# A hybrid decoder step: stream buffers and gate matrices allocated later, attention emitted in larger steps

## The chip, the cores and the metric

The kernel runs on one core of one Trainium2 chip. The metric is the device time of one execution in microseconds (us). The kernel before was timed three times: 1510.71, 1504.4 and 1509.47 us, so the median is 1509.47 us. One more execution was profiled: it took 1513.5 us, of which the trace covers a span of 1511.7 us.

Engines are named as the profile names them: PE is the matrix engine (PEld its weight loads), DVE the vector engine, ACT the scalar engine, POOL GpSimd, SP the engine that here only issues transfers.

## The reference, cut to what matters

One layer for 256 prompt tokens and 32 new tokens of 8 running sequences (288 columns in all):

```
h = RMSNorm(x);  [p_rwkv | lru_x | lru_gate | q | k | v] = h @ W_in
y = concat(RWKV7(p_rwkv), RGLRU(lru_x, lru_gate), DilatedWindowAttn(q, k, v)) @ W_out
x = x + RMSNorm(y)
x = x + RMSNorm(relu(RMSNorm(x) @ W1)^2 @ W2)
```

The attention has 8 heads of 128 numbers and a bias that depends on the distance of query and key alone. For the prompt it is a block form: query block 0 sees key block 0, query block 1 sees key blocks 0 and 1. For the running sequences it reads 896 of the 2048 cached keys and values of each sequence, those that the dilated windows reach. The RWKV part has 8 heads of 64 in two halves of four; a half is a chain of small dependent matrix products.

## The kernel before, in words

**Dense work.** Every weight chunk of 512 KB is loaded by SP, split by ACT and DVE into a high and a low part (L385, L386, three ring slots), and multiplied on PE three times (L421 high by high, L422 high by low, L423 low by high). One such product with 288 columns is called a dense matmul here. The input projection has 46 output tiles of 48 dense matmuls each (2208 in all); then the output projection runs in four passes of 192 (R, L, G0, G1: the RWKV part, the LRU part, heads 0 to 3, heads 4 to 7), then the feed-forward layer with 6144. Places in the program are given as *tile 29*, that is, after 29 x 48 dense matmuls, counted on from the input projection into the passes, so that pass R begins at tile 46, L at 50, G0 at 54, G1 at 58.

**Mixers.** What lies between the projections (RWKV, LRU, attention) is written as Python generators. While the dense work is emitted, `pump` runs them a step at a time within a budget, so that their instructions stand between the dense ones; a scheduler then sets the final order on every engine, and each engine runs its own list in that order. Before a pass the program drains the generators that the pass needs. `yield 0.85` tells `pump` what a step costs.

**RWKV.** `gen_rwkv(hf)` prepares half `hf`; `gen_form` makes its 64 x 64 products; `gen_inv` inverts blocks on DVE and turns them by a round trip through DRAM (DVE copy L851, out with L854, back with L859, all on SP's queue), whose result PE needs in `gen_mats` (L888). `gen_chain`, `gen_rwkv_sample` and `gen_gn` follow. The constant `GATE` names the key of half 0 that half 1 waits for before it starts at all: `Q1`, set when half 0 has finished the second of its two `gen_mats`.

**Cached keys and values.** `gen_sample_scores` takes 32 batches of keys of 896 KB (L1365, issued by POOL, four matmuls L1395 each), `gen_sample_pv` 32 half batches of values of 1024 or 768 KB (L1458, 28 matmuls L1479 for a whole batch). They share four stream buffers: two in `arm` and two taken from the arena at the start (`ar` in the trace). POOL issues in order: a load whose buffer isn't free holds up what stands behind it.

**Prompt attention.** `gen_prompt_attn` runs head by head. The bias is a table by distance; a load gives it in the order of growing distance, so that it is turned around on PE by two transposes with a reversed identity (`jm`, L1544) and evicted by ACT (L1545), then scores (L1555, L1556), softmax, three transposes (L1576). `gen_prompt_pv` turns the values (L1593) and multiplies (L1600, L1601), head by head.

**The end.** After the last column sums (`sum_cols`, L404) and ahead of the last scaling stands a loop of 72 matmuls (L1814) whose results nobody reads.

Of the kernel before, what the change touches and what calls it, by code (L numbers as in the profile page):

```python
# [17 lines left out]
NT = NP_ + NS  # L18
# [33 lines left out]
GATE = 'Q1'  # L52
# [41 lines left out]
def _consts():  # L94
# [50 lines left out]
    return ca, cb, oh_p, ln_p, oh_s, ln_s, np.eye(128, dtype=np.float32)[::-1].copy()  # L145
# [17 lines left out]
def prepare(inputs):  # L163
# [58 lines left out]
    a["c_a"], a["c_b"], a["c_ohp"], a["c_lnp"], a["c_ohs"], a["c_lns"], a["c_j"] = _consts()  # L222
# [89 lines left out]
def build(tc, A, O):  # L312
    nc = tc.nc
    sy, dv, ac, po, pe = nc.sync, nc.vector, nc.scalar, nc.gpsimd, nc.tensor
    with ExitStack() as ctx:
# [337 lines left out]
        def gen_rwkv(hf):  # L653
# [528 lines left out]
        def gen_lru():  # L1182
# [3 lines left out]
            gt = yield from aw(2, 4, 128)  # L1186
            sy.dma_start(out=gt, in_=A["gates"])
# [25 lines left out]
            yield 0  # L1213
            while 0 not in xbt:
                yield 0
# [83 lines left out]
        def evac_qkv(which, i, ps):  # L1299
# [5 lines left out]
            QKV[which, i] = t  # L1305
            S[which + "n"] = i + 1
# [3 lines left out]
        def gen_tables():  # L1310
# [17 lines left out]
            jm = yield from aw(128)  # L1328
            sy.dma_start(out=jm, in_=A["c_j"])
            S["jm"] = jm  # L1330
# [21 lines left out]
        def gen_sample_scores():  # L1352
# [3 lines left out]
            def pre(n):  # L1356
                for i in range(n):
# [13 lines left out]
            for g in range(2):  # L1371
# [12 lines left out]
                for hf in range(2):  # L1384
                    bh, = yield from bk(1)
                    for b in range(NB):
                        i = (g * 2 + hf) * NB + b
                        pre(i + 1 + LAG)
                        yield from take()
                        while i not in kst:  # L1390
                            yield 0
                            pre(i + 1)
                        t, buf = kst[i]
                        for h in range(4):
                            pe.matmul(out=bh[32 * h:32 * h + 32, 0:448], lhsT=qz[:, h, b], rhs=t[:, h],  # L1395
                                      start=(b == 0), stop=(b == NB - 1))
                        streams.append(buf)
                        kst[i] = None
                        yield 0.85
# [43 lines left out]
        def gen_sample_pv():  # L1443
# [3 lines left out]
            def pre(n):  # L1447
                for i in range(n):
# [12 lines left out]
            for g in range(2):  # L1461
# [4 lines left out]
                for b in range(NB):  # L1466
                    bb, = yield from bk(1)
                    for kg in range(2):
                        i = (g * NB + b) * 2 + kg
                        pre(i + 1 + LAG)  # L1470
                        yield from take()
                        while i not in vst:
                            yield 0
                            pre(i + 1)
                        t, buf = vst[i]
# [6 lines left out]
                        vst[i] = None  # L1482
                        if kg == 0:
                            yield 1.2
# [6 lines left out]
                    yield 1.0  # L1491
# [30 lines left out]
        def gen_prompt_attn():  # L1522
            while "dtab" not in S:
                yield 0
            d0, jm = S["dtab"], S["jm"]
            hbs = {}

            def load(h):
                t = yield from aw(2, 128)
                for i in range(2):  # L1530
                    po.dma_start(out=t[:, i], in_=bass.AP(tensor=d0.tensor, offset=d0.offset + 384 * h + 1 + 128 * i,
                                                          ap=[[1, 128], [1, 128]]))
                hbs[h] = t

            yield from load(0)
            for _ in range(6):
                yield 0
            for h in range(8):
                TB = yield from aw(256)
                if h < 7:  # L1540
                    yield from load(h + 1)
                b, = yield from bk(1)
                for i in range(2):
# [3 lines left out]
                arena.put(hbs.pop(h))  # L1547
                while ("k", h) not in QKV:
                    yield 0
                qt, kt = QKV.pop(("q", h)), QKV.pop(("k", h))  # L1550
                P = yield from aw(3, 128)
                s_ = yield from aw(8)
                yield 0.2
                b, = yield from bk(1)
                pe.matmul(out=b[:, 0:128], lhsT=qt[:, 0:128], rhs=kt[:, 0:128], start=True, stop=True)  # L1555
                pe.matmul(out=b[:, 128:384], lhsT=qt[:, 128:256], rhs=kt[:, 0:256], start=True, stop=True)  # L1556
                near, far = TB[:, 0:128], TB[:, 128:256]
                for blkq, tb in ((0, near), (1, far), (2, near)):
                    dv.scalar_tensor_tensor(out=P[:, blkq], in0=b[:, 128 * blkq:128 * blkq + 128], scalar=SCALE, in1=tb,
                                            op0=ALU.mult, op1=ALU.add)  # L1560
                banks.put(b)
                arena.put(TB, qt, kt)
                sls = (slice(0, 1), slice(1, 3))
                for i, sl in enumerate(sls):
                    dv.tensor_reduce(out=s_[:, i:i + 1], in_=P[:, sl], axis=mybir.AxisListType.XY, op=ALU.max)
                dv.tensor_scalar(out=s_[:, 0:2], in0=s_[:, 0:2], scalar1=-1.0, scalar2=None, op0=ALU.mult)
                for i, sl in enumerate(sls):
                    ac.activation(out=P[:, sl], in_=P[:, sl], func=AF.Exp, bias=s_[:, i:i + 1], accum_out=s_[:, 2 + i:3 + i])
                dv.reciprocal(out=s_[:, 4:6], in_=s_[:, 2:4])
                for i, sl in enumerate(sls):  # L1570
                    dv.tensor_scalar(out=P[:, sl], in0=P[:, sl], scalar1=s_[:, 4 + i:5 + i], scalar2=None, op0=ALU.mult)
                yield 0.7
                PT = yield from aw(3, 128)
                b, = yield from bk(1)
                for i in range(3):
                    pe.transpose(b[:, 128 * i:128 * i + 128], P[:, i], ident)  # L1576
                ac.activation(out=PT, in_=b[:, 0:384].rearrange("p (a b) -> p a b", a=3), func=AF.Copy)
                banks.put(b)
                arena.put(P, s_)
                QKV["p", h] = PT  # L1580
                yield 0.4
            arena.put(jm)

        def gen_prompt_pv():
            outs = {}
# [255 lines left out]
```

## Time and profile before

| | |
|---|---|
| three runs | 1504.4 to 1510.71 us, median 1509.47 us |
| the profiled execution: its time, its span | 1513.5 us, 1511.7 us |
| PE | busy 1447.7 us (96% of the span) |
| PEld | 1358.9 us (90%) |
| DVE | 837.0 us (55%) |
| ACT | 604.2 us (40%) |
| POOL | 80.1 us (5%) |
| HBM | 268.03 MB read, 6.84 MB written, 182 GB/s over the span |
| the chain that ended last | PE 90%, DMA 4%, DVE 3%, ACT 1%, issue 1% |

The averages hide stages. The profile's view in 40 slices has a slice of 37.8 us each; the feed-forward layer fills the slices from 18 on evenly, and slices 12 and 13 (from about 453 to 529 us) stand out on PE, on PEclk (the granted clock of PE, 9 for full speed, 5 for half) and on DMA. A matmul's end is modelled, so a busy PE says how long it had work in flight, not that it ran at its peak; the rate of the dense matmuls is the better measure.

### The profile page before, as it was taken

The page shows a single profiled execution, that of the slowest core. Times are in us where ns is not written, and L with a number is a line of the kernel's source. Part 1 is how long each engine was busy: PE and PEld are TensorE (multiplying, and loading weights), DVE is VectorE, ACT ScalarE, POOL GpSimd, SP SyncE. Part 2 cuts the span into 40 slices and gives each one's busy share as a digit, 9 for nine tenths or more (in the row PEclk, how much of TensorE's full clock was granted, in tenths as well). Part 3 has the DMA queues.
Part 4 walks back from the last instruction along what each step waited for, and adds up shares of the span by engine and source line. Part 5 has one row for each costly group of instructions (what it writes and reads, how often), then busy time and mean ns, then how long its engine had stood idle before and what let it go on. Part 6 is the DMA issues. An engine that isn't in the chain of part 4 may idle for free.

```text
span 1511.7 us, 28221 instructions
## 1 busy us (share of the span) xinstructions
PE 1447.7 (96%) x11802; PEld 1358.9 (90%) x11802; DVE 837.0 (55%) x1415; ACT 604.2 (40%) x880; POOL 80.1 (5%) x167
## 2 busy tenths in 40 slices
PE   9998999999997769999999999999999999999997
PEld 8897778778886439999999999999999999999996
DVE  7785348447775146679443345544455544455554
ACT  7432325334433114366443344433344433444442
POOL 3101012121111000000000000000000000000000
PEclk9999999999998559999999999999999999999998
DMA  8656576787986114534544444444454454444452
GB/s 302 180 158 197 184 286 229 266 337 269 348 265 208 41 34 167 183 126 154 163 162 166 167 166 168 166 165 165 164 165 167 168 167 165 164 162 165 168 168 77
DMA packets 86319, 276.70 MB, mean 183 GB/s; under 512 B 22528, under 2 KB 26288, under 8 KB 84144
## 3 DMA queue, kind: packets, MB, share of 16 engines
q1 hardware_dynamic: 75280, 212.30, 41.4%
q0 software_dynamic: 10048, 60.84, 11.3%
q8 instruction: 92, 1.51, 0.4%
q10 hardware_dynamic: 864, 1.77, 0.3%
q14 instruction: 35, 0.29, 0.1%
HBM read 268.03 MB, written 6.84 MB: 182 GB/s over the span
## 4 chain that ended last, share of the span: by engine, by line
PE 90%; DMA 4%; DVE 3%; ACT 1%; issue 1%; POOL 0%; SPq 0%; DVEq 0%; ACTq 0%; POOLq 0%
PE mm L421 26%; PE mm L422 26%; PE mm L423 26%; PE bt L1479 2%; PE bt L1395 2%; DMA ar<-do 1%; DMA w<-in_w_in 1%; DMA ar<-dtab 1%; DMA o_v<-ar 1%; DMA arm<-in_vc 1%; PE bt L965 0%; PE bt L1070 0%; PE bt L1083 0%; DVE arm L1818 0%; DMA ar<-dm 0%
## 5 line engine op out<-in xcount | busy, mean ns | idle before, releaser
L386 DVE TENSOR_TENSOR ring_l<-w,ring_h 128x1024 fp32r<-128x1024 f32 (+1 forms) x382 | 465.2, 1218 | 395.1 <-ACT ring_h L385 392.7
L385 ACT ACTIVATE ring_h<-w 128x1024 fp32r<-128x1024 f32 (+1 forms) x382 | 403.0, 1055 | 578.1 <-PE mm L422 528.5
L421 PE MATMUL mm<-hh,ring_h 128*128 128x288 f32 x1984 | 598.8, 302 | 3.8 <-ACT ring_h L385 2.0
L422 PE MATMUL mm<-hl,ring_h 128*128 128x288 f32 x1984 | 592.7, 299 | 0.2 <-DVE hl L540 0.2
L423 PE MATMUL mm<-hh,ring_l 128*128 128x288 f32 x1984 | 589.9, 298 | 0.0
L421 PEld LDWEIGHTS mm<-hh,ring_h 128*128 128x128 f32 x1984 | 374.5, 189 | 15.2 <-issue 8.3
L423 PEld LDWEIGHTS mm<-hh,ring_l 128*128 128x128 f32 x1984 | 375.4, 189 | 6.9 <-issue 5.2
L422 PEld LDWEIGHTS mm<-hl,ring_h 128*128 128x128 f32 x1984 | 375.1, 189 | 5.4 <-issue 3.1
L422 PE MATMUL mm<-fl,ring_h 128*128 128x288 f32 x1024 | 302.1, 295 | 0.0
L423 PE MATMUL mm<-fh,ring_l 128*128 128x288 f32 x1024 | 301.9, 295 | 0.0
L421 PE MATMUL mm<-fh,ring_h 128*128 128x288 f32 x1024 | 300.3, 293 | 0.0
L421 PEld LDWEIGHTS mm<-fh,ring_h 128*128 128x128 f32 x1024 | 192.5, 188 | 0.0
L422 PEld LDWEIGHTS mm<-fl,ring_h 128*128 128x128 f32 x1024 | 192.5, 188 | 0.0
L423 PEld LDWEIGHTS mm<-fh,ring_l 128*128 128x128 f32 x1024 | 192.4, 188 | 0.0
L1781 ACT ACTIVATE fh<-ft 128x288 fp32r<-128x288 f32 x64 | 28.3, 445 | 78.9 <-DVE ft L1780 78.9
L1789 DVE TENSOR_TENSOR arm<-mm,arm 128x288 f32<-128x288 f32 x48 | 22.0, 458 | 51.1 <-PE mm L423 51.1
L1782 DVE TENSOR_TENSOR fl<-ft,fh 128x288 fp32r<-128x288 f32 x64 | 29.2, 458 | 29.2 <-ACT fh L1781 29.2
L1780 DVE SCALAR_TENSOR_TENSOR ft<-mm,rt 128x288 f32<-128x288 f32 x63 | 28.3, 450 | 0.0
L1779 ACT ACTIVATE rt<-mm 128x288 f32<-128x288 f32 x63 | 24.9, 395 | 0.4 <-PE mm L423 0.4
L1479 PE MATMUL bt<-arm,ar 128*32 128x128 f32 x472 | 19.2, 317 | 5.4 <-DVE ar L848 2.5
L1479 PEld LDWEIGHTS bt<-arm,ar 128*32 128x32 f32 x472 | 14.7, 126 | 8.1 <-DVE ar L848 2.7
L1688 DVE TENSOR_TENSOR ar<-mm,ar 128x288 f32<-128x288 f32 x32 | 14.6, 455 | 8.8 <-PE mm L423 8.8
(438 smaller groups left out, 992.9 us busy)
## 6 DMA issues: line engine op xcount, KB each, us to landing
w<-in_w SPq DMA_DIRECT2D x256, 512.0 KB
w<-in_w_in SPq DMA_DIRECT2D x91, 512.0 KB
w<-in_w_out SPq DMA_DIRECT2D x32, 512.0 KB
arm<-in_kc POOLq DMA_DIRECT2D x16, 896.0 KB, 6.6
ar<-in_kc POOLq DMA_DIRECT2D x16, 896.0 KB, 7.6
ar<-in_vc POOLq DMA_DIRECT2D x8, 1024.0 KB, 7.0
arm<-in_vc POOLq DMA_DIRECT2D x8, 1024.0 KB, 6.5
arm<-in_vc POOLq DMA_DIRECT2D x9, 768.0 KB, 6.8
```

The costliest lines, as they stand in the source:

```text
L385: ac.activation(out=h[:, lo:hi], in_=t[:, lo:hi], func=AF.Copy)
L386: dv.tensor_tensor(out=l[:, lo:hi], in0=t[:, lo:hi], in1=h[:, lo:hi].bitcast(F32), op=ALU.subtract)
L421: pe.matmul(out=ps, lhsT=h, rhs=xh, start=start, stop=False)
L422: pe.matmul(out=ps, lhsT=h, rhs=xl, start=False, stop=False)
L423: pe.matmul(out=ps, lhsT=l, rhs=xh, start=False, stop=stop)
L1395: pe.matmul(out=bh[32 * h:32 * h + 32, 0:448], lhsT=qz[:, h, b], rhs=t[:, h], start=(b == 0), stop=(b == NB - 1))
L1479: pe.matmul(out=bb[32 * h:32 * h + 32, 0:128], lhsT=PT[:, kt, 32 * h:32 * h + 32], rhs=t[:, q, h], start=(kt == 0), stop=(kt == 6))
L1779: ac.activation(out=r, in_=ps, func=AF.Relu)
L1780: dv.scalar_tensor_tensor(out=f, in0=ps, scalar=0.0, in1=r, op0=ALU.max, op1=ALU.mult)
L1781: ac.activation(out=fh[:, m], in_=f, func=AF.Copy)
L1782: dv.tensor_tensor(out=fl[:, m], in0=f, in1=fh[:, m].bitcast(F32), op=ALU.subtract)
L1789: dv.tensor_tensor(out=facc[:, m], in0=ps, in1=facc[:, m], op=ALU.add)
```

## The change

- **RWKV half 1 starts earlier.** `GATE` becomes `TQ`, the key that half 0 sets when its inversion has been emitted.
- **Stream buffers late.** At the start there are only the two in `arm`. `more_streams` takes the other two from the arena once half 1 of RWKV has its last large buffer (the key `held`).
- **Gate matrices late.** `gen_lru` takes memory for the gate matrices and loads them once the first tile of values has left PE (the key `late`).
- **Cached keys in twos.** `gen_sample_scores` waits for two batches and emits their eight matmuls in one step; each of the two stands for one `take`.
- **Cached values by batch.** `gen_sample_pv` waits for both halves of a batch and emits its 28 matmuls in one step.
- **Prompt heads in pairs, keys backwards.** The bias is loaded for two heads by two transfers of 128 KB and used as it comes: the scores are made with the keys in reverse (`kt[:, 127::-1]`), and the softmax's last step writes them forwards again. `jm`, its two transposes per head and the eviction are gone. Softmax and values run two heads at a time; a head's product with the values is three matmuls of 128 columns (before: one of 256 and one of 128).
- **The loop of 72 matmuls at the end is gone.**

```diff
-GATE = 'Q1'
+GATE = 'TQ'
-        streams = [arm[:, 0:2304], arm[:, 2304:4608]] + [arena.get(2048, top=True) for _ in range(NSTR)]
-        strx = streams[2:]
+        streams = [arm[:, 0:2304], arm[:, 2304:4608]]
+        strx = []
+        def more_streams():
+            while "held" in RS[1] and len(strx) < NSTR:
+                t = arena.get(2048, top=True)
+                if t is None:
+                    return
+                strx.append(t)
+                streams.append(t)
...
             MV = yield from aw(2, NT, top=True)
+            R["held"] = True
...
+            while "late" not in S:
+                yield 0
+            gt = yield from aw(2, 4, 128)
+            sy.dma_start(out=gt, in_=A["gates"])
...
-                    for b in range(NB):
-                        i = (g * 2 + hf) * NB + b
-                        pre(i + 1 + LAG)
-                        yield from take()
-                        while i not in kst:
+                    for b2 in range(0, NB, 2):
+                        i = (g * 2 + hf) * NB + b2
+                        for _ in range(2):
+                            yield from take()
+                            pre(i + 2 + LAG)
+                        while i not in kst or i + 1 not in kst:
                             yield 0
...
-                b, = yield from bk(1)
-                for i in range(2):
-                    pe.transpose(b[:, 128 * i:128 * i + 128], hbs[h][:, i], jm)
-                ac.activation(out=TB, in_=b[:, 0:256], func=AF.Copy)
...
+                    pe.matmul(out=b[:, 0:128], lhsT=qt[:, 0:128], rhs=kt[:, 127::-1], start=True, stop=True)
+                    pe.matmul(out=b[:, 128:384], lhsT=qt[:, 128:256], rhs=kt[:, 255::-1], start=True, stop=True)
...
-        for n, K in ((6, 128), (6, 64), (6, 32), (6, 128), (6, 32)):
-            for i in range(n):
-                for r in range(128 // K):
-                    pe.matmul(out=bt[:, r, 0:NT], lhsT=ring_h[K * r:K * r + K, 0, i], rhs=F["h"][K * r:K * r + K, i],
-                              start=True, stop=True)
```

The order on the engines moves at three places. Line numbers of the changed program are eight higher up to the attention, then more.

PE, pass R just after the input projection, before. L1083 to L1151 are the last steps of RWKV half 1, and the rows above them are the same kind of work with few dense matmuls between:

```order
L1003 MATMUL bt<-ar_88 64x64 x4
L1083 MATMUL bt<-ar_88 64x64 x4
L1098 MATMUL bt<-ca,ar_88 64x32 x4
L1128 MATMUL bt<-ar_88,ca 128x288 x2
L1135 MATMUL bt<-ar_88,ca 128x288 x2
L1110 MATMUL bt<-ar_88 64x512 x2
L1151 MATMUL bt<-ar_88 128x288 x2
L421 MATMUL mm<-hh,ring_h 128x288 x3
L422 MATMUL mm<-hl,ring_h 128x288
```

The same pass in the changed program; L1494 are a batch of cached values, L429 to L431 the dense matmuls:

```order
L429 MATMUL mm<-hh,ring_h 128x288
L430 MATMUL mm<-hl,ring_h 128x288
L431 MATMUL mm<-hh,ring_l 128x288
L1494 MATMUL bt<-ar_88 32x128 x16
L1494 MATMUL bt<-arm,ar_88 32x128 x12
L429 MATMUL mm<-hh,ring_h 128x288
```

What moved: from tile 45.9 to tile 46.6 PE's list holds 347 mixer matmuls in the program of before and 4 in the changed one. There RWKV half 1 ends at tile 39.6, the LRU's last gate products stand at 43.4, and the last batch of values at tile 50.0.

PE, the first matmuls of RWKV half 1 that need the round trip through DRAM, in the changed program (L1445 is the softmax of the cached scores, L897 the consumer of the round trip, L1561 and L1562 scores of prompt heads):

```order
L431 MATMUL mm<-hh,ring_l 128x288
L1445 MATMUL bt<-ca,arx 128x128 x4
L897 MATMUL bt<-ar_88 64x64 x16
L1561 MATMUL bt<-ar_88,arx 128x128
L1562 MATMUL bt<-ar_88,arx 128x256
```

They stood at tile 44.9 and stand at tile 29.0 now. Between VectorE's copy that starts the round trip and the consumer, PE's list holds 65 dense matmuls in the program of before (for either half) and 41 dense and 14 other matmuls for half 1 in the changed one (66 dense for half 0).

POOL, the loads of cached keys for heads 0 to 3, before (L1304 is the copy that belongs to the eviction of a tile):

```order
L1365 DMA arm<-in_kc 128x1792
L1304 COPY arx<-ar_88 128x32
L1365 DMA arm<-in_kc 128x1792
L1365 DMA ar_88<-in_kc 128x1792 x2
L1304 COPY arx<-ar_88 128x32
L1365 DMA arm<-in_kc 128x1792
```

and in the changed program:

```order
L1315 COPY arx<-ar_88 128x32 x2
L1376 DMA arm<-in_kc 128x1792 x4
L1315 COPY arx<-ar_88 128x32
L839 MEMSET ar_88 128x1024
L1376 DMA arm<-in_kc 128x1792 x2
L1315 COPY arx<-ar_88 128x32
L1376 DMA arm<-in_kc 128x1792 x2
```

All 32 key batches go through the two buffers in `arm` now; the loads into the other two begin at tile 35.4, with values. The pairs of key batches stand at tiles 20.2, 21.4, 22.3, 22.9, 24.2, 25.2, 26.0 and 27.2, then (after one batch of values at 29.5 in the same two buffers) at 30.3, 30.9, 31.8, 33.0, 34.1, 34.8, 35.6 and 36.3.

## Rows read from the trace of the kernel before

**Rows 1.** The page, 40 slices: busy tenths of PE, granted clock.

```profile
PE   9998999999997769999999999999999999999997
PEclk9999999999998559999999999999999999999998
```

**Rows 2.** Stretches: start:end us, length, busy of each engine (instructions), clock, DMA.

```profile
core 0: us, PE busy (x) PEld busy (x) DVE busy (x) ACT busy (x) POOL busy (x), PEclk, DMA share, GB/s
149.00:252.60 103.60, 103.48 (x995) 77.81 (x994) 55.99 (x120) 36.24 (x60) 18.35 (x36) 1.00 0.68 245
252.60:451.00 198.40, 190.46 (x1876) 161.74 (x1874) 130.84 (x306) 77.25 (x132) 33.20 (x66) 0.98 0.81 286
463.50:565.00 101.50, 69.55 (x706) 46.28 (x705) 39.51 (x103) 20.84 (x48) 3.60 (x8) 0.61 0.25 81
565.00:660.00 95.00, 95.00 (x708) 93.91 (x708) 64.41 (x102) 45.35 (x69) 0.00 (x0) 1.00 0.50 168
680.00:1490.00 810.00, 810.00 (x6102) 809.79 (x6102) 407.16 (x483) 342.52 (x452) 0.00 (x0) 1.00 0.48 162
```

**Rows 3.** The same view, two short stretches behind waits.

```profile
140.00:160.00 20.00, 18.84 (x229) 16.84 (x230) 6.62 (x12) 5.42 (x10) 1.55 (x3) 0.86 0.46 158
320.00:340.00 20.00, 18.11 (x125) 14.06 (x117) 6.38 (x14) 6.21 (x13) 3.86 (x6) 0.91 0.80 291
```

**Rows 4.** PE groups, 463.5 to 565 us: count, busy, mean ns, idle before.

```profile
L1479 PE MATMUL bt<-arm,ar 128*32 128x128 f32 x136 | 7.3, 387 | 1.3 <-ACT ar L920 0.5 <-ACT ar L966 0.5 <-DVE ar L1041 0.4
L1479 PE MATMUL bt<-ar 128*32 128x128 f32 x112 | 5.2, 349 | 1.0 <-ACT ar L1245 1.0
```

**Rows 5.** PE groups, 149 to 252.6 us.

```profile
L422 PE MATMUL mm<-hl,ring_h 128*128 128x288 f32 x129 | 40.8, 316 | 0.0
L423 PE MATMUL mm<-hh,ring_l 128*128 128x288 f32 x129 | 40.0, 310 | 0.0
L421 PE MATMUL mm<-hh,ring_h 128*128 128x288 f32 x128 | 39.6, 310 | 0.0
```

**Rows 6.** The chain that ended last, pieces: start us, us, what.

```profile
204.48 0.89 PE bt L1395 x8
375.83 1.01 PE bt L1479 x32
```

**Rows 7.** PE's waits in the whole span: us in total, times, longest.

```profile
PE bt L888 <- DMA ar<-do: 6.7, 1, 6.7
PE bt L1395 <- ACT ar L1545: 1.9, 1, 1.9
PE bt L1544 <- DMA ar<-dtab: 1.5, 2, 1.1
```

**Rows 8.** VectorE's copies that start the two round trips: start, us.

```profile
126.85 0.37 DVE L851 COPY ar<-ar 64x256 f32<-64x256 f32 x1
...
442.50 0.39 DVE L851 COPY ar<-ar 64x256 f32<-64x256 f32 x1
```

**Rows 9.** The chain behind the first round trip, and SP's issues of the second.

```profile
127.54 2.41 DMA do<-ar
131.60 9.41 DMA ar<-do
141.15 0.45 PE bt L888 x2
...
447.32 3.77 SPq L859 DMA_DIRECT2D ar<-do  x8
```

**Rows 10.** The line of key loads: POOL's time of one, and landing.

```profile
L1365 POOL DMA_DIRECT2D arm<-in_kc x16: 530/530/536, 128.7 to 315.6; - x16
...
DMA to landing us min/median/max: 4.6/7.4/12.1
```

**Rows 11.** PE forms of the bias transposes and of the scores: ns min, median, max.

```profile
L1544 PE MATMUL bt<-arx,ar x14: 272/328/331, 250.3 to 340.4; 128*128 128x128 f32 x14
...
L1556 PE MATMUL bt<-ar x8: 379/380/382, 274.4 to 345.6; 128*128 128x256 f32 x8
```

**Rows 12.** The end of the kernel in time: ACT's last square, then PE.

```profile
1494.02 0.44 ACT L1792 ACTIVATE sqt<-arm 128x288 f32<-128x288 f32 x1 [5.33 <-DVE arm L1789]
...
1494.13 1.36 PE L1814 MATMUL bt<-fh,ring_h 128*128 128x288 f32 x8
1495.43 0.83 PE L404 MATMUL mm<-ca,sqt 128*128 128x1 f32 x6
```

More of the change, by code (lines that the diff above doesn't have):

```diff
@@ L144, in _consts @@
     ln_s = np.tile(ln_s, (4, 1))
-    return ca, cb, oh_p, ln_p, oh_s, ln_s, np.eye(128, dtype=np.float32)[::-1].copy()
+    return ca, cb, oh_p, ln_p, oh_s, ln_s
 OUTS = {
@@ L1305, in evac_qkv @@
             QKV[which, i] = t
+            if which == "v":
+                S["late"] = True
             S[which + "n"] = i + 1
@@ L1385, in gen_sample_scores @@
                     bh, = yield from bk(1)
-                    for b in range(NB):
-                        i = (g * 2 + hf) * NB + b
-                        pre(i + 1 + LAG)
-                        yield from take()
-                        while i not in kst:
-                            yield 0
[L1392 to L1399, printed above, removed]
+                    for b2 in range(0, NB, 2):
[4 more added lines that the diff above has]
+                        while i not in kst or i + 1 not in kst:
+                            yield 0
+                            pre(i + 2)
+                        for b in (b2, b2 + 1):
+                            t, buf = kst[i + b - b2]
+                            for h in range(4):
+                                pe.matmul(out=bh[32 * h:32 * h + 32, 0:448], lhsT=qz[:, h, b], rhs=t[:, h],
+                                          start=(b == 0), stop=(b == NB - 1))
+                            streams.append(buf)
+                            kst[i + b - b2] = None
+                        yield 1.7
                     sl = SS[:, g, 448 * hf:448 * hf + 448]
@@ L1467, in gen_sample_pv @@
                     bb, = yield from bk(1)
-                    for kg in range(2):
[L1469 to L1475, printed above, removed]
+                    i = (g * NB + b) * 2
+                    for _ in range(2):
+                        yield from take()
+                        pre(i + 2 + LAG)
+                    while i not in vst or i + 1 not in vst:
+                        yield 0
+                        pre(i + 2)
+                    for kg in range(2):
+                        t, buf = vst[i + kg]
                         for q in range((4, 3)[kg]):
@@ L1524, in gen_prompt_attn @@
                 yield 0
[L1525 to L1526 removed]
+            d0 = S["dtab"]
+            tabs = {}
             def load(h):
[L1529 to L1535 removed]
@@ L1582, in gen_prompt_attn @@
[L1582 to L1602 removed]
+                t = yield from aw(2, 2, 128)
@@ new lines, in gen_prompt_pv @@
+        def gen_prompt_pv():
+            for h0 in range(0, 8, 2):
+                while ("v", h0 + 1) not in QKV or ("p", h0) not in QKV:
+                    yield 0
+                PT = QKV.pop(("p", h0))
+                VP = yield from aw(2, 2, 128)
+                b, = yield from bk(1)
+                for e in range(2):
+                    vt = QKV.pop(("v", h0 + e))
+                    for j in range(2):
+                        pe.transpose(b[:, 256 * e + 128 * j:256 * e + 128 * j + 128], vt[:, 128 * j:128 * j + 128], ident)
+                    arena.put(vt)
+                ac.activation(out=VP, in_=b.rearrange("p (e j d) -> p e j d", e=2, j=2), func=AF.Copy)
+                banks.put(b)
+                yield 0.6
+                o0 = yield from att_out(h0)
+                o1 = yield from att_out(h0 + 1)
+                b, = yield from bk(1)
+                for e in range(2):
+                    o = 256 * e
+                    pe.matmul(out=b[:, o:o + 128], lhsT=VP[:, e, 0], rhs=PT[:, e, 0], start=True, stop=True)
+                    pe.matmul(out=b[:, o + 128:o + 256], lhsT=VP[:, e, 0], rhs=PT[:, e, 2], start=True, stop=False)
+                    pe.matmul(out=b[:, o + 128:o + 256], lhsT=VP[:, e, 1], rhs=PT[:, e, 1], start=False, stop=True)
+                for e, oh in enumerate((o0, o1)):
+                    ac.activation(out=oh[:, 0:256], in_=b[:, 256 * e:256 * e + 256], func=AF.Copy)
```

125 lines of the change are left out of this document (53 added, 72 removed).

## The prediction, made before the changed kernel ran

> **What bounds the kernel now.** I read the 40 slices first. PE is at 9 nearly throughout, but slices 12 and 13 show 7 on PE and 8 and 5 on its clock [rows 1]. Then the stretches [rows 2]: in the feed-forward layer PE runs 6102 matmuls in 810.00 us, 0.1327 us each, at clock 1.00. Nothing in the change touches that, so over half of the time is fixed. The stretch from 463.5 to 565 us is the other extreme: 101.50 us long, PE busy 69.55 us, clock 0.61, which is a mix of its two levels of 2.4 and 1.2 GHz. In it PE runs only 31 dense matmuls; the rest is RWKV half 1, some four batches of cached values, four prompt heads and the LRU's last product. Here nothing is full: DVE is busy 39.51 us, the DMA share is 0.25. PE waits for short dependent steps, 32 us in all, and the idle time brings the low clock, so that the steps themselves take twice as long. The same steps for RWKV half 0 stand from 149 to 252.6 us between dense matmuls, and there PE is busy 103.48 of 103.60 us at clock 1.00 [rows 2]. So the bound of this stretch is the latency of a chain with no dense work to fill its gaps. That is what the moved `GATE` changes: in the new order half 1 ends at tile 39.6, well inside the input projection, and the value batches run on to tile 50.0 inside the passes that don't need them.
>
> **The change part by part.** All sums are against the profiled execution, 1513.5 us.
>
> *The pile-up.* The work stays on PE's list; what goes is idle time and low clock. At full clock it would cost at least 69.55 x 0.61 = 42.4 us [rows 2]. From the other side I price it by half 0: 103.60 us less 386 dense matmuls [rows 5] at 0.1327 us (51.2) leaves 52.4 us; in it are 16 key batches at 0.89 us [rows 6], 14.2 us, and about 2 us of other products, so half 0 cost 36 us. Part of half 1's first products had run before 463.5 us (about 2.5 us), so 33.5. To that come 31 dense matmuls (4.1), 248 records of values, where 32 took 1.01 us, so 8 [rows 4, 6], and prompt heads and LRU (5): 50.6 us. I take 46.5, the middle, as neither side is nearer. The pile-up gives back 55 us (bounds 51 and 59).
>
> *The second round trip.* For half 0, PE needs the result at 141.15 us, and the copy ends at 127.22, so the trip takes 13.9 us [rows 8, 9]; 65 dense matmuls (8.6 us) stand in between, and PE waits 6.7 us [rows 7]. In the program of before half 1 had as much cover and no long wait: its copy ends at 442.89, SP issues the last return at about 451.1 [rows 8, 9], so a trip of over 8.2 us with less traffic. In the new order half 1 has 41 dense matmuls (5.4 us) and 14 others, about 1.7 us: 7.1 us. PE, which takes its list in order, waits between 1 and 6.8 us there with all dense work behind it. I take 5. Behind half 0's wait the clock is 0.86 over 20 us [rows 3], which costs 2.8 us; I add 3. Together +8 (0 to 10).
>
> *Keys and values.* A pair holds both buffers until its own matmuls are through. From its start to the next pair's data pass 2 x 0.89 us, POOL's 0.53 us and a landing of 7.4 us (4.6 to 12.1) [rows 6, 10]: 9.7 us. Half 0's stretch ran 8.05 tiles in 103.60 us, 12.9 us a tile [rows 2, 5], so the pairs' distances of 0.63 to 1.25 tiles are 8.1 to 16 us, and of the 15 pairs that follow another batch three wait, 0.5 to 1.6 us each: +3. One pair (tile 34.1) is late for another reason: its loads stand on POOL's list behind the copy of a tile evicted at 33.5. With that, and some value batches that stand half a tile apart at tile 40, I take +6 in all, clock included (0 to 61, the upper end under the rivals).
>
> *The bias.* 16 transposes leave PE, 0.33 us of span each but overlapped [rows 11], about 2 us; the 1.5 us wait for the table goes, and the 1.9 us wait of a key batch behind ACT's eviction L1545 [rows 7], with the clock of 0.91 about it, 1.8 us [rows 3]. The table's load still has to land, but at a DVE instruction now. I take -5 (0 to -7). Reversed keys and the reversed write change an address step alone; no row shows such an access. Between nothing and a doubling of the 16 score matmuls at 0.33 to 0.38 us a span [rows 11], 5 us, I take 0, as the count of columns is the same. Eight more value matmuls: +1.
>
> *The end.* ACT's square is ready at 1494.46; PE's sums of it start at 1495.43, behind eight of the unread matmuls [rows 12]. That is -0.9; the other 64 stand where the scaling or DVE's tail is later anyway.
>
> *Late buffers and gate matrices, other load.* The gate load lands some tiles ahead of its use at tile 38: nothing. DVE takes 39.51 us more into the mixed part [rows 2]: 55.99 + 130.84 + 39.51 = 226.3 us of some 350 us, 65%, so it isn't the bound on the mean; for local queues +2. What is late next: R, L and G0 have their inputs 2.6 tiles and more ahead, G1 7 tiles.
>
> Sum: -55 + 8 + 6 - 5 + 1 - 0.9 + 2 = -44, so 1469.5 us for an execution like the profiled one. The median of the three runs stands at 1509.47/1513.5 = 0.9973 of it: 1465 us.
>
> **The rivals.**
>
> *DVE or the chains bind in places.* In the new order half 1's shift mixing stands about tile 21 and the LRU about tile 40, both long on DVE, beside the splits that DVE owes the dense work. Already in the stretch from 252.6 to 451 us DVE is busy 66%, and PE is idle 7.94 us [rows 2]. If PE waits there as long as half of the pile-up's 32 us of idle time [rows 2], 16 us, and 4 us of clock follow, the gain is 24 us: 1485. For it: half 1 is a chain of small steps with the same latencies as before. Against it: half 0's stretch has 0.12 us of idle time.
>
> *Slower: the key pairs serialise.* A load that always lands in 12.1 us, the longest seen [rows 10], makes a pair's cycle 14.4 us. Summed over the distances, ten of the pairs then wait 43 us, and behind each wait comes low clock, 1.8 us each as about 320 us [rows 3], 18 us: 61 instead of the 6 in the sum, so +11, 1520 us. It decides from a landing of about 11 us on. Against it: such landings came where four loads were queued at once, and now there are never more than two.
>
> The Trainium skill speaks for this rival in Trainium Kernel Development and Optimization, Best Practices: double-buffer, so that loads overlap with compute. A pair that takes both buffers isn't double-buffered. By that rule the waits are those of this rival; by the rows the next pair stands far enough behind that dense work covers the load, and the sum keeps +6. TensorE: Matmul & The Clock Gate, the section on HAM oscillation, adds that a loop with a transfer wait in every step runs every step cold, as the clock of 0.86 and 0.91 behind two waits here has it for single ones.
>
> *Nothing is gained.* The change could leave the pile-up if memory ran out and a drain emptied the generators at the end of the projection. The new order speaks against it: 4 mixer matmuls stand there.
>
> *More is gained.* The lower price of the pile-up, no new waits and the bias at its best: -59 - 7 - 0.9 = -67, 1443 us.
>
> **How the numbers follow.** The forecast, 1465, has a chance of 0.65; DVE and chains, 1485, 0.18; more, 1443 to 1450, 0.10; nothing 0.03; slower 0.04. The range of 8 in 10 goes from 1445 (most of the better case) to 1489 (the DVE rival with a little more wait); it leaves out the last two cases and the edges. About 0.5%, 7.5 us, is what a measurement of this kernel can tell from no change. Faster by more: 0.93; within: 0.03; slower: 0.04.
>
> **What would show it.** In the new profile slices 12 and 13 read 9 on PE and on the clock, no stretch of over 20 us has a clock below 0.8, and pass R's dense run begins between 500 and 510 us instead of about 564 us. A wait of L897 for the round trip of 1 to 7 us right or wrong shows the second term; the waits of L1408 and L1494 for loads in `arm` the third: over 20 us and I was wrong about the pairs. If PE's idle time between tiles 18 and 46 is over 20 us with DVE as releaser, the first rival has it. The prediction as a whole is wrong if RWKV half 1 still runs after the last input tile, or if PE is busy there and yet the dense matmuls are slow.

## The result and the profile after

The changed kernel takes 1457.17 us (median of four runs, 1456.77 to 1457.5); the kernel before took 1508.89 us beside it (four runs). The ratio is 0.9661, with a 95% interval of 0.964 to 0.9683. The forecast was 1465 us with a range from 1445 to 1489. The profiled execution took 1457.43 us with a span of 1455.4 us, 56.3 us less than the span of before.

The page of the changed kernel in 40 slices (of 36.4 us), busy tenths of PE and granted clock, answering [rows 1]:

```profile
PE   8998999899999999999999999999999999999995
PEclk9999999899999999999999999999999999999998
```

The hole of 7 on PE and 8 and 5 on the clock is gone. On the clock one 8 is left, in the eighth slice (255 to 291 us).

Where the time went can be read between dense matmuls that both programs have in the same places (tile starts, worked out from the starts of the dense matmuls). Up to the start of tile 18 the changed kernel is 1.3 us ahead (147.7 against 149.0). From there to tile 46 it takes longer, 349.1 against 316.1 us, because RWKV half 1 and the prompt heads stand there now. From tile 46 to 51 it takes 42.9 against 130.0 us. So tiles 18 to 51 take 392.1 instead of 446.1 us, -54.0. The feed-forward layer takes the same, and the end is 0.9 us shorter. The whole stretch in one row, before (start:end, length, busy of PE, PEld, DVE, ACT, POOL, clock, DMA share, GB/s):

```profile
149.00:595.10 446.10, 406.08 (x3970) 325.91 (x3969) 250.30 (x565) 152.99 (x271) 55.89 (x112) 0.90 0.63 220
```

and after:

```profile
147.70:539.80 392.10, 379.61 (x3971) 315.95 (x3970) 245.93 (x539) 143.43 (x255) 49.10 (x105) 0.98 0.70 253
```

PE is idle 446.10 - 406.08 = 40.0 us before and 12.5 us after, and the mean clock rises from 0.90 to 0.98. No matmul went away to speak of: the rows count 3970 and 3971 records.

What PE waits for in the changed kernel, from 120 to 160 us (total, times, longest), answering [rows 7]:

```profile
PE bt L897 <- DMA ar<-do: 4.3, 1, 4.3
```

from 260 to 310 us:

```profile
PE bt L1445 <- DVE arx L1437: 2.0, 1, 2.0
PE bt L897 <- ACT ar L1447: 0.7, 1, 0.7
PE bt L1561 <- DVE ar L1565: 0.7, 1, 0.7
PE bt L897 <- DVE ar L898: 0.6, 1, 0.6
PE bt L1561 <- DVE ar L898: 0.5, 1, 0.5
```

and the loads of keys (L1408) and values (L1494) in the whole span:

```profile
PE bt L1494 <- DMA ar<-in_vc: 3.1, 1, 3.1
...
PE bt L1408 <- DMA arm<-in_kc: 2.3, 3, 1.1
...
PE bt L1494 <- DMA arm<-in_vc: 1.1, 1, 1.1
```

The first two lists hold a surprise: the 4.3 us for the round trip through DRAM are the first trip's, at 139 us, where the kernel before waits too (6.7 us). For the second trip, about 280 us, PE does not wait at all.

### The profile page after: what moved, and what is told of

Its sections match the earlier page's. It is cut to its first block, busy times and chain, and to the rows that moved or that the text cites. A ratio compares the mean times of both kernels' runs of the same rounds, so it can differ in the third digit from the quotient of the medians.

```text
span 1455.4 us, 28004 instructions
## 1 busy us (share of the span) xinstructions
PE 1415.3 (97%) x11730; PEld 1342.6 (92%) x11730; DVE 834.7 (57%) x1399; ACT 595.9 (41%) x866; POOL 67.5 (5%) x159
## 4 chain that ended last, share of the span: by engine, by line
PE 70%; issue 2%; DVE 2%; DMA 2%; ACT 1%; POOL 0%; DVEq 0%; POOLq 0%
PE mm L429 22%; PE mm L431 22%; PE mm L430 22%; DMA arm<-in_vc 1%; PE bt L1494 1%; DMA arm<-in_kc 1%; PE bt L1408 0%; DVE arm L1827 0%; DVE arx L1828 0%; PE bt L425 0%; DVE ring_l L394 0%; ACT ring_h L393 0%; DMA w<-in_w_out 0%; PE bt L1612 0%; ACT L1277 0%
## 5 line engine op out<-in xcount | busy, mean ns | idle before, releaser
L429 PE MATMUL mm<-hh,ring_h 128*128 128x288 f32 x1984 | 598.7, 302 | 4.8 <-ACT ring_h L393 3.0
L431 PE MATMUL mm<-hh,ring_l 128*128 128x288 f32 x1984 | 592.1, 299 | 0.8 <-DVE ring_l L394 0.8
L429 PEld LDWEIGHTS mm<-hh,ring_h 128*128 128x128 f32 x1984 | 373.7, 188 | 15.9 <-issue 7.1
L431 PEld LDWEIGHTS mm<-hh,ring_l 128*128 128x128 f32 x1984 | 374.8, 189 | 9.7 <-issue 5.5
L431 PE MATMUL mm<-fh,ring_l 128*128 128x288 f32 x1024 | 301.9, 295 | 0.0
L429 PE MATMUL mm<-fh,ring_h 128*128 128x288 f32 x1024 | 300.3, 293 | 0.0
L429 PEld LDWEIGHTS mm<-fh,ring_h 128*128 128x128 f32 x1024 | 192.5, 188 | 0.0
L431 PEld LDWEIGHTS mm<-fh,ring_l 128*128 128x128 f32 x1024 | 192.4, 188 | 0.0
L1408 PE MATMUL bt<-arm,ar 128*32 128x448 f32 x256 | 28.0, 546 | 2.6 <-DMA arm<-in_kc 2.3
L1376 POOL DMA_DIRECT2D arm<-in_kc x32 | 17.0, 531 | 70.2 <-PE bt L1408 61.4
```

Source lines behind the costliest of these rows:

```text
L429: pe.matmul(out=ps, lhsT=h, rhs=xh, start=start, stop=False)
L431: pe.matmul(out=ps, lhsT=l, rhs=xh, start=False, stop=stop)
L1376: after(po.dma_start(out=t, in_=A["kc"][seq[i]]), S["mark"])
```

## The experiments

All ratios are to the kernel before, run on the same chip beside each. Four questions were asked.

### What dissolved the pile-up: the gate or the memory

The prediction credits `GATE`. But the trace of before has two rows that speak against it. L664 makes the first products of an RWKV half, L806 its 64 x 64 products; these are half 1's (count, ns min/median/max, first and last start):

```profile
L664 PE MATMUL bt<-ar x4: 402/454/507, 164.3 to 171.7; 64*128 64x288 f32 x4
```

```profile
L806 PE MATMUL bt<-ar x64: 267/267/321, 371.9 to 377.6; 64*64 64x128 f32 x64
```

Half 1 began at 164.3 us, long before the pile-up, and then took 208 us to its next large products. `GATE` has no part in that stretch. The rival theory: half 1 could not get its buffers, because two stream buffers had taken 4096 columns of the arena from the start. Five kernels tell the two apart.

**late_streams_alone**, before with the late stream buffers and nothing else:

```diff
-        streams = [arm[:, 0:2304], arm[:, 2304:4608]] + [arena.get(2048, top=True) for _ in range(NSTR)]
-        strx = streams[2:]
+        streams = [arm[:, 0:2304], arm[:, 2304:4608]]
+        strx = []
+        def more_streams(): ...          # as in the change, called from both pre()
...
+            R["held"] = True
```

> The kernel before with one edit: the two arena stream buffers are taken only once half 1 of RWKV has its last large buffer. GATE stays at Q1, and everything else is as before. Theory G (the prediction's: the moved GATE dissolves the pile-up): the pile-up between 463.5 and 565 us stays, about 1505 us. Theory M (the pile-up was a lack of memory: half 1 could not get its buffers while the streams held 4096 columns of the arena): half 1 ends at about tile 41 instead of 46.4, pass R runs dense, and of the 51.7 us gained in all at least 45 come: 1457 to 1466 us, with some waits for single key batches.

Measured: 1462.96 us, ratio 0.967 (0.9637 to 0.9702). Its page and its rows for half 1:

```profile
PE   8998999979999999999999999999999999999997
PEclk9999999979999999999999999999999999999999
```

```profile
L672 PE MATMUL bt<-ar x4: 402/455/507, 165.0 to 172.4; 64*128 64x288 f32 x4
```

```profile
L815 PE MATMUL bt<-ar x64: 267/267/321, 259.4 to 265.6; 64*64 64x128 f32 x64
```

Half 1 starts at the same time as before (165.0, with the old gate) and has its products 112 us earlier. This one edit is worth 47 of the 52 us.

**gate_alone**, before with `GATE = 'TQ'`:

```diff
-GATE = 'Q1'
+GATE = 'TQ'
```

> The kernel before with one edit: GATE is TQ. Theory G: half 1 starts earlier and so ends inside the input projection, 1455 to 1470 us. Theory M: half 1 starts earlier and then waits for memory all the same; its last steps still stand in pass R, the slices 12 and 13 stay low: 1495 to 1515 us.

Measured: 1552.74 us, ratio 1.0271 (1.0224 to 1.0317), slower than both theories had it.

```profile
PE   8998989999994757999999999999999999999997
PEclk9998989999995556999999999999999999999999
```

```profile
L806 PE MATMUL bt<-ar,arx x64: 267/267/321, 421.7 to 433.6; 64*64 64x128 f32 x64
```

Half 1 starts 14 us earlier (150.0 us) and gets to the same products 50 us *later*. The hole is four slices long now. That half 1 holds what it has while it lacks the rest, and so starves the others as well, fits this, but is only argued.

**memory_held**, late_streams_alone with the memory taken away again, though no load uses it:

```diff
+        idle = [arena.get(2048, top=True) for _ in range(2)]
         def more_streams():
-            while "held" in RS[1] and len(strx) < NSTR: ...
+            return
```

> late_streams_alone with one difference: two blocks of 2048 columns of the arena are taken at the start and lie idle until the cached values are done, and no third or fourth stream buffer is ever made. So the loads go through two buffers as in late_streams_alone, but the memory is as short as in the kernel before. Theory M (memory): RWKV half 1 starves, the pile-up is back, 1500 to 1515 us, PE and clock low in slices 12 and 13. Rival S (late streams help because the loads of keys and values are fewer at a time or later): about 1463 us as in late_streams_alone.

Measured: 1526.81 us, ratio 1.0106 (1.0066 to 1.0147).

```profile
PE   8998999989998669999999999999999999999997
PEclk9999999999999559999999999999999999999999
```

```profile
L811 PE MATMUL bt<-ar x64: 267/267/321, 381.6 to 387.3; 64*64 64x128 f32 x64
```

The hole is back though the loads go through two buffers. It is the memory, not the loads. The theory of the gate falls. The rows also show a place where half 1 stands still. Behind its first products it takes two buffers of 1152 columns each together, and VectorE's first write to one of them (`AR`) comes at 314.5 us before, at 219.0 us in late_streams_alone and at 331.2 us in memory_held, while the first products stand at 164.3, 165.0 and 163.3 us. (In gate_alone that write comes at 220.5 us, and half 1 stands still behind it.)

**gate_back** (the changed kernel with `GATE = 'Q1'`) and **streams_early** (the changed kernel with all four buffers from the start) ask the same from the other side:

```diff
-GATE = 'TQ'
+GATE = 'Q1'
```

> The changed kernel with GATE back at Q1. Theory G: the pile-up is back, about 1500 us. Theory M: half 1 starts later but ends at tile 41.6, no pile-up: 1455 to 1462 us; the second round trip then has another cover, so that its wait of 4.3 us may go or grow by some 3 us.

```diff
-            while "held" in RS[1] and len(strx) < NSTR:
+            while len(strx) < NSTR:
...
+        more_streams()
         NU = KT // 2
```

> The changed kernel with all four stream buffers from the start, as before the change; GATE is TQ. Theory G: no pile-up, about 1457 us or a little better, since key pairs then have four buffers. Theory M: half 1 again ends in pass R at tile 46.4, with a stretch of low clock there: 1490 to 1510 us.

Measured: gate_back 1464.47 us, ratio 0.9688 (0.9662 to 0.9715); streams_early 1472.6 us, ratio 0.9741 (0.9698 to 0.9783). Without the moved gate 46 us of the gain are there. With early buffers 38 of the 52 us are there too, which neither theory had. So the late buffers are enough for most of the gain, but they are not the only way to much of it. The change also takes the 1024 columns of the gate matrices later and does without the 128 of `jm`, so it may be memory here too; which of the other edits does it was not tried apart. In streams_early half 1 has its products at 284.3 us (228.7 in the changed kernel), and what piles up at tile 46 (48.8 us beyond its dense matmuls) is mostly batches of values (392 of the 469 other matmul records there).

### Which start of half 1 is best, once the memory is there

**gate_earlier**, the changed kernel with

```diff
-GATE = 'TQ'
+GATE = 'MA0'
```

> The changed kernel with GATE at MA0, so that RWKV half 1 starts when half 0 has its first masked products: its second round trip is needed at tile 26.0 instead of 29.0, its last step stands at 36.2 instead of 39.4. With the late buffers in place, Q1 gave 1464.5 and TQ 1457.2 us. Theory E (earlier is better as long as memory is there): 1450 to 1456 us. Rival (once nothing piles up, only the local waits differ): 1456 to 1463 us, with PE idle plus clock loss between tiles 18 and 51 of about 20 us as in the changed kernel.

Measured: 1443.53 us, ratio 0.955 (0.952 to 0.958). This is faster than the changed kernel, whose interval begins at 0.964. Tiles 18 to 51:

```profile
148.80:525.10 376.30, 372.85 (x3962) 313.27 (x3961) 242.38 (x528) 138.90 (x248) 50.15 (x105) 0.99 0.74 263
```

PE is idle 3.5 us in it instead of 12.5. Half 1 has its products at 195.4 us.

**no_gate**, with `GATE = None`:

> The changed kernel without any gate: RWKV half 1 starts as soon as its inputs are there and runs beside half 0. Half 0's products behind the first round trip then stand at tile 18.9 instead of 17.4, and half 1 ends at tile 33.6 (36.2 in gate_earlier, 39.4 in the changed kernel). In gate_earlier PE is idle only 3.5 us between tiles 18 and 51, so little is left there; the wait of 4 to 7 us for the first round trip is what could still go. Theory E (earlier is better as long as memory is there): 1435 to 1443 us. Rival (two halves at a time hold so much memory that keys or values start late and pile up in the passes, where 28 mixer matmuls stand at the end of the projection and the last values at tile 52): 1446 to 1460 us.

Measured: 1481.5 us, ratio 0.9816 (0.9777 to 0.9855): slower again, and not as the rival had it. Nothing piles up at the end; two stretches in the middle stall.

```profile
PE   8999969979899999999999999999999999999995
PEclk9999979989999999999999999999999999999998
```

The 6 in the sixth slice is a wait of 10.8 us, from 186.2 to 197.0 us, that ends with half 1's round trip. The first 4.3 us of it are not the trip: VectorE's copy that starts the trip comes only at 190.55 us, at the end of the inversion. The two halves run side by side, and PE's list has no other matmul left between that copy and L897. So by the medians "earlier is better" holds from Q1 over TQ to MA0 (1464, 1457, 1444 us) and not beyond, though the intervals of the first two overlap (0.9662 to 0.9715 and 0.964 to 0.9683). The gate decides what stands beside what; against the changed kernel it is worth 14 us one way and 24 us the other.

### What the added waits cost

**trip_late** puts more dense work ahead of the second round trip's consumer:

```diff
             while "TQ" not in R:
                 yield 0
+            if hf:
+                for _ in range(4):
+                    yield 0
```

> The changed kernel, with one edit: gen_mats of RWKV half 1 lets four more steps of the pump pass before it emits the products that need the second round trip; they stand at tile 29.9 instead of 29.0, with some 42 more dense matmuls (5.6 us) ahead of them. Theory T (the 4.3 us wait of L897 and the low clock behind it cost what they show, some 4.3 us of idle time plus about 5 us of clock between 280 and 300 us): the wait is gone or under 1 us, the stretch from 280 to 300 us reads a clock of 1.00, and the time falls by 5 to 9 us against the changed kernel's 1457.2, to 1448 to 1452 us. Rival (the wait only moves: half 1 ends later, and the value batches at tiles 39 to 41 or the LRU wait instead): 1455 to 1460 us.

Measured: 1461.41 us, ratio 0.9685 (0.9647 to 0.9722), no gain. The expectation rests on a misreading: it takes the 4.3 us wait of the whole span for the second trip's. In trip_late it is still there, at 120 to 160 us (3.8 us), as it belongs to half 0. What the changed kernel waits for at 281 us is a row of short steps (start, us, what, in brackets the idle time before and its releaser):

```profile
281.04 0.88 PE L1445 MATMUL bt<-ca,arx 128*128 128x128 f32 x4 [1.98 <-DVE arx L1437]
...
282.67 1.29 PE L897 MATMUL bt<-ar 64*64 64x64 f32 x16 [0.75 <-ACT ar L1447]
...
284.54 1.12 PE L897 MATMUL bt<-ar 64*64 64x64 f32 x16 [0.59 <-DVE ar L898]
...
286.19 0.80 PE L1561 MATMUL bt<-ar,arx 128*128 128x128 f32 x2 [0.53 <-DVE ar L898]
...
288.56 0.79 PE L1561 MATMUL bt<-arx 128*128 128x128 f32 x2 [0.71 <-DVE ar L1565]
```

Softmax of the cached scores, RWKV products and scores of prompt heads follow each other with almost no dense matmul between, each waiting for DVE or ACT. By the time PE gets to L897 the trip's data have come: VectorE's copy starts at 272.2 us, so the trip took under 10.5 us. The stretch from 280 to 300 us, and two more, the dense run of pass R and the 20 us behind the waits of the value batches:

```profile
280.00:300.00 20.00, 16.34 (x184) 13.75 (x186) 9.46 (x25) 5.71 (x16) 1.50 (x4) 0.74 0.39 133
```

```profile
497.00:560.00 63.00, 62.76 (x645) 60.47 (x645) 33.95 (x53) 25.00 (x40) 2.86 (x6) 1.00 0.74 261
440.00:460.00 20.00, 18.87 (x226) 17.23 (x227) 15.47 (x49) 9.76 (x13) 3.51 (x8) 0.87 0.87 324
```

In the first of them PE is idle for 3.7 us and the mean clock is 0.74, a mix of the levels of 2.4 and 1.2 GHz, which by estimate costs up to another 5 us (20 us x 0.26). In trip_late a knot stands at the same place without the RWKV products (softmax, scores of prompt heads and values), with 4.0 us idle and the same clock:

```profile
280.00:300.00 20.00, 15.99 (x136) 11.86 (x138) 6.13 (x18) 4.42 (x13) 3.11 (x7) 0.74 0.60 197
```

**first_trip_late** covers the trip that PE does wait for: the same edit with `if not hf` and seven steps.

> The changed kernel with one edit: gen_mats of RWKV half 0 lets seven steps of the pump pass before it emits the products that need the first round trip. They stand at tile 18.4 instead of 17.4, with 48 more dense matmuls (6.3 us) ahead, which is more than the 4.3 us that PE waits there. Theory T (a wait for the round trip costs its idle time and the low clock behind it, 0.88 over 20 us): the wait goes, the clock from 140 to 160 us reads 0.95 or more, and the time falls by 4 to 7 us: 1450 to 1453 us. Rival (what follows half 0 only shifts by a tile and waits elsewhere, as with trip_late): 1456 to 1462 us.

Measured: 1466.63 us, ratio 0.9696 (0.9663 to 0.9728). No gain, perhaps a loss (the intervals overlap), though the first half of theory T is right:

```profile
140.00:160.00 20.00, 20.00 (x239) 16.02 (x239) 12.60 (x20) 7.51 (x12) 2.78 (x7) 1.00 0.66 228
...
280.00:300.00 20.00, 12.38 (x142) 9.83 (x140) 7.32 (x13) 5.19 (x9) 1.07 (x2) 0.73 0.43 142
300.00:320.00 20.00, 14.61 (x151) 10.42 (x155) 4.29 (x14) 2.56 (x8) 3.52 (x9) 0.59 0.33 110
```

The wait is gone, the clock behind it is 1.00, and tile 18 starts at 140.8 us instead of 147.7. All of it, and more, goes at tile 29, which takes 40.5 us (13.4 in the changed kernel): the knot again, now with 13 us of idle time and a clock of 0.73 and 0.59. The edit that gained 7 us locally moved every generator behind it to another place: half 1's first products, for one, stand at 117.5 us instead of 148.2.

**batches_single** has the keys one batch at a time and the values half a batch at a time, as before (`for b in range(NB)`, `yield 0.85`; `yield 1.2` between the halves).

> The changed kernel with the cached keys one batch at a time and the values half a batch at a time, as before; all else, the late stream buffers too, as changed. The larger steps were put at +6 us (waits of pairs). Theory P (pairs cost what their waits show): the 2.3 us of L1408 and the 4.2 us of L1494 go, and the time is 2 to 7 us below 1457.2: 1450 to 1455 us. Rival (single batches wait as much, since the same two buffers serve them, and each brings its own switch between dense and other matmuls): 1457 to 1465 us.

Measured: 1461.91 us, ratio 0.9685 (0.9647 to 0.9723). Its waits for keys are 0.8 us and for values 2.2 us, against 2.3 and 4.2, and yet tile 51 starts 2.6 us later. The two ratios overlap, so the larger steps are worth nothing that these runs resolve, in either direction; a cost of 6 us is not what they show.

### The small terms

**bias_turned** brings the transposes and the eviction back, for two heads at a time. In this kernel the near and the far key block of query block 1 stay exchanged on the way to the product with the values; the work is the same.

```diff
+                for e in range(2):
+                    for i in range(2):
+                        pe.transpose(b[:, 256 * e + 128 * i:256 * e + 128 * i + 128], t[:, e, i], jm)
+                ac.activation(out=TB, in_=b.rearrange("p (e i d) -> p e i d", e=2, i=2), func=AF.Copy)
...
-rhs=kt[:, 255::-1]
+rhs=kt[:, 0:256]
```

> The changed kernel with the bias turned around on PE as before: four transposes for a pair of heads, one eviction by ACT, keys and softmax forwards. Heads stay in pairs. Theory B (the term of -5, 0 to 7): 1459 to 1464 us, with PE waits for ACT's eviction at the transposes or the steps behind it. Rival (the transposes and the eviction fit beside the dense work, and the gain of the term came from elsewhere): 1456 to 1459 us.

Measured: 1459.76 us, ratio 0.9669 (0.9634 to 0.9704), between the two theories and not resolved. That reversed access costs nothing here is shown by rows instead. The score matmul with the keys backwards, eight of the sixteen, beside the 379/380/382 ns of L1556 in [rows 11]:

```profile
L1562 PE MATMUL bt<-arx,ar x8: 379/380/382, 313.2 to 336.1; 128*128 128x256 f32 x8
```

As a matmul's end is modelled, the starts say more: the trace has two records of each such matmul, and at full clock the second starts 0.22 us behind the first, backwards as forwards.

VectorE's last step of the softmax reads its operand backwards now (`in0=P[:, e, sl, ::-1]`); it does not write backwards, as the prediction has it:

```profile
L1579 DVE TENSOR_SCALAR arx<-ar,arx x8: 278/316/349, 294.6 to 319.9; 128x128 f32<-128x128 f32 x4, 128x256 f32<-128x256 f32 x4
```

The same step forwards, before:

```profile
L1571 DVE TENSOR_SCALAR ar<-ar,arx x14: 278/346/392, 248.3 to 333.7; 128x128 f32<-128x128 f32 x7, 128x256 f32<-128x256 f32 x7
```

These medians mix two shapes. The 128x256 ones alone take 344 to 349 ns backwards and 346 to 350 ns forwards.

**tail_kept** keeps the loop of 72 unread matmuls.

> The changed kernel with the loop of 72 unread matmuls at the end kept. By the term of the tail it is 0.9 us slower, 1458.1 us, too little for these rounds; in the trace the sums of ACT's last square then start about 1 us behind that square instead of at once. Rival (all 72 stood in time that is idle anyway): the end of the trace is the same to 0.2 us.

Measured: 1459.04 us, ratio 0.9665 (0.9624 to 0.9706). The trace resolves what the times can't. ACT's last square and PE's sums of it in the changed kernel, answering [rows 12], and then in tail_kept:

```profile
1438.60 0.44 ACT L1806 ACTIVATE sqt<-arm 128x288 f32<-128x288 f32 x1 [5.33 <-DVE arm L1803]
...
1439.09 0.83 PE L412 MATMUL mm<-ca,sqt 128*128 128x1 f32 x6 [0.24 <-ACT sqt L1806]
```

```profile
1439.40 1.36 PE L1828 MATMUL bt<-fh,ring_h 128*128 128x288 f32 x8
1440.69 0.83 PE L412 MATMUL mm<-ca,sqt 128*128 128x1 f32 x6
```

In tail_kept the square ends at 1439.72 us, so the sums start 0.97 us behind it (0.05 in the changed kernel), and from the square's start to the end of the span it takes 1.0 us longer.

## Why the prediction was right, and where it was not

**The time.** 1457 us is inside the range and 8 us below the forecast. The gain in the medians is 51.7 us, in the profiled executions 56.3, the forecast had 44.

**The cause: wrong.** The step that failed is in the first part: "That is what the moved `GATE` changes". The order of the changed program was right, half 1 does end at tile 39.6, but the reason is the memory that the late stream buffers leave free. Late buffers alone give 47 us, the gate alone costs 43 us. (That the other edits reach 38 us without late buffers stays open.) The prediction counted the late buffers under other load, at nothing, and named memory only in the rival in which nothing is gained. The two rows on L664 and L806 stood in the trace of before and would have told it. The forecast came out because it priced the order of the changed program as a whole, whatever had brought that order about. With the cause wrong that is luck: the same reasoning put gate_alone at 1455 to 1470 us, and it took 1552.74.

**The pile-up: right in kind, too small.** It was put at -55 us, since the work would cost 46.5 us elsewhere (at least 42.4). gate_earlier has the same work almost without waits, so it prices it: 376.3 us, less 3.5 us idle, less 2 to 6 us for a clock of 0.99, is 367 to 371 us for tiles 18 to 51. Before, the same tiles without the pile-up's 101.5 us [rows 2] take 344.6 us, with 8.1 us idle and 3 to 5 us lost at the clock of 0.98 between 252.6 and 451 us [rows 2]: 331 to 334 us. So the moved work costs an estimated 33 to 40 us, and the pile-up gives back 61 to 68 (what the changed bias saves of PE's work is in this too, put at 2 us in the prediction). The mistake is in both bounds: 69.55 us busy times the clock of 0.61 was taken as the least that the work can cost, but busy time counts how long a matmul is in flight (a record of a 128x256 score matmul lasts 380 ns, and the next starts after 218), and in a row of waiting steps little overlaps it. Why the other bound, by half 0's 36 us, is too high as well is not shown.

**The second round trip: right in size, wrong in mechanism.** No wait for the trip appears (the prediction had 1 to 7 us). In its place stands the knot of short steps at 281 us: 3.7 us idle and up to 5 us of clock, where the term had 5 and 3. That the sizes agree is luck. A wait for the second trip, 4.8 us, does appear in gate_back, at tile 30.6.

**Keys and values: right.** Three of the pairs were to wait, 0.5 to 1.6 us each; L1408 waits three times, 1.1 us at most (the pair at tile 34.1, which the prediction names), 2.3 us in all. The value batches at tile 40 wait 3.1 and 1.1 us, and the clock behind is 0.87 over 20 us. With up to 2.6 us for that it is about 9 us, 6 were taken. In batches_single such waits are 3.0 us instead of 6.5 and the time is no shorter, so these runs don't show the term to be the price of the pairs. The rival in which pairs serialise needed landings of 11 us; the page has a median of 7.3 us for the 32 loads.

**All added waits together** were +12 us (8 + 6 - 5 + 1 + 2). After takes 392.1 us where the work without waits takes 367 to 371, before lost 11 to 13 us outside the pile-up: a net 8 to 14 us. So the sum of these terms holds within what can be told, and the 11 us by which tiles 18 to 51 beat the forecast (-54 against -43) fit the 6 to 13 us by which the pile-up was put too small.

**The bias** was put at -5. Its two waits are gone, 1.2 us of waits for L1565 and L898 stand at L1561; bias_turned bounds it to a few us and doesn't fix it. **The end**: -0.9 taken, 0.9 to 1.0 measured.

**What would show it.** Pass R's dense run begins at 496.8 us, a little before the 500 to 510 that were given, and slices 12 and 13 read 9. One sign failed by a little: from 280 to 304 us, 24 us, the clock is 0.79. PE's idle time from tile 18 to 51 is 12.5 us, and the longest wait with DVE as releaser is 2.0 us, so the rival of DVE and chains didn't come about in the changed kernel; first_trip_late comes nearer to it, with a wait of 5.0 us for DVE at L1448.

The Trainium skill's rule (Trainium Kernel Development and Optimization, Best Practices: double-buffer, so that loads overlap with compute) doesn't hold as a reason against this change. The two further buffers let loads run further ahead, but held the memory that a chain on the path needed; giving them up until late gained 47 us and cost 2.0 and 1.1 us of waits for loads in late_streams_alone.

## What to carry to other kernels

Before a gain is credited to a flag that starts work earlier, look when that work starts now, and how long it takes from one of its steps to a later one: the 208 us here, 94 us with the memory free, were a sign that the chain lacked something, here memory that prefetch buffers held from the start. On-chip memory is a resource of the schedule like an engine, and a buffer that is taken late can be worth more than a load that is issued early. Where one list of instructions feeds a busy engine, a wait of 4 to 7 us that is taken out can come back elsewhere, so try several starts of the same chain (here 1444 to 1481 us) and keep the one whose stretch has the least idle time.

## What the runs showed of the hardware

The wait for the first round trip through DRAM is not the same in kernels whose lists are the same up to there: 4.3 us in the changed kernel, 3.8 in trip_late, 4.6 in tail_kept, 5.5 in batches_single. Over all kernels here in which it stands at tile 17 it is 3.8 to 7.8 us. So a part of the 2.4 us by which it shrank (6.7 to 4.3) may be no effect of the change.

Short waits cost clock as well as time. Waits of 2.0 us and less, with few dense matmuls between (the knot at 281 us), went with a granted clock of 0.74 over 20 us; in first_trip_late, 13 us of idle time in 40 us went with 0.73 and 0.59.

An operand read backwards, the moving one on PE or VectorE's input, took no longer than forwards (for 128x256, the records of a matmul start 0.22 us apart either way at full clock, and VectorE takes 344 to 349 ns against 346 to 350).
